# Own buffers for the weights a layer's last tiles read twice, the next layer's first splits on VectorE, and four tiles by halves at the end of the first attention

## The chip, the cores and the metric

One core of a Trainium2 chip runs the whole program. The metric is device time in microseconds (us) for one execution, as the median of several; lower is better. The engines are TensorE (PE, with its weight loads PEld), VectorE (DVE), ScalarE (ACT), GpSimd (POOL) and SyncE (SP, which issues most of the DMAs). Each engine takes its instructions in the order in which the program lists them.

## What is computed

One sequence of 512 positions, model width 1024, fp32, goes through two layers and a third, hybrid layer. Every layer starts from a normed and modulated copy of `x`, and ends by adding a gated product to `x`:

```python
for i in range(2):
    h = rms_norm(x, norm_mix[i]) * (1 + sc1) + sh1
    y = chunked_relpos_attention(h, ...) if i == 0 else chunked_spatial_gating(h, ...)
    x = x + g1 * y
    h = rms_norm(x, norm_ffn[i]) * (1 + sc2) + sh2
    x = x + g2 * squared_relu_mlp(h, ffn_w1[i], ffn_w2[i])      # hidden width 4096
return hybrid_layer(x, ...)      # block-sparse attention beside a state-space mixer, own norm at its start
```

So there are four layer ends inside the program, at which a norm over all of `x` stands between the last product of one half layer and the first product of the next: attention to feed-forward 0, feed-forward 0 to spatial gating, spatial gating to feed-forward 1, feed-forward 1 to the hybrid layer.

## The kernel before

`x` is held transposed as eight tiles `xT[k]` of 128 features by 512 positions. Every large product is made of three reduced-precision products (`mm3`, lines 147 to 152): each operand is split into a rounded part and its remainder, for activations `hH` and `hL`, for weights `wh` and `wl`. A weight chunk is read and split by `wchunk` (line 154): SP loads it into `raw` (four buffers), ScalarE rounds it into `wh` (line 163, three buffers), and VectorE or GpSimd subtracts to give `wl` (line 168, three buffers). Which of the two subtracts follows a running count, unless the caller names an engine.

At a layer's end `down_last` (line 336) makes the last four of eight output tiles. Tile 4 is made over all 512 positions. Tiles 5, 6 and 7 are made for the first 256 positions and then, from the same weights, for the other 256; so three `wh` and three `wl` buffers, which is all there are, stay taken until the second halves are done. `resid` (line 325) adds each product to `xT` on VectorE.

Into this is woven the next layer's norm, a generator (`norm`, line 249) that `down_last` steps: squares of the first five tiles on ScalarE (line 257) summed on GpSimd (line 261); for each half of the positions the squares of the last three (line 270) with two more sums (line 272), column sums by small products with ones (line 275), the mean (line 278), an inverse root `rsqrt` (line 171), two transposes that spread it over the partitions (line 282), and then `norm_tile` for each feature tile: line 315 on VectorE, line 316 on ScalarE (`hH`), line 317 on VectorE (`hL`). `rsqrt` is a bit trick and three Newton rounds, ten small VectorE instructions (lines 181 to 185); with `act=True` it is Ln and Exp on ScalarE (lines 178, 179) and one Newton round of three.

The next layer's first products are made by `up_first` (line 364) in steps of two feature tiles and a half of the positions, in the order SKEW (line 93): (0,0), (1,0), (0,1), (2,0), (1,1), (3,0), (2,1), (3,1). It splits four weight chunks, the first on VectorE and the other three on GpSimd. All four layer ends use both functions.

The order of instructions on each engine is set when the program is built, by a scheduler that simulates the engines and places what it thinks is ready, by priority; the norm's steps run at high priority. Buffers are rings: an instruction that writes one waits until its last readers are done. In the first attention `relb` and `P3` hold four position-bias tiles and four probability tiles; in the gating layer `v0` to `v3` hold the gated values; beside the second feed-forward the state-space tables are made in `s5_tab`, `s5_ct` and `s5_c9` and stored to DRAM (line 1003).

Of the kernel before, what the change touches and what calls it, by code (L numbers as in the profile page):

```python
# [19 lines left out]
T = 512  # L20
# [89 lines left out]
class Net:  # L110
# [42 lines left out]

    def wchunk(self, src, k, n, eng=None):

        nc = self.nc
        raw = self.wp.tile([128, 1024], F32, name="raw", tag="raw", bufs=4)
        wh = self.wp.tile([128, 1024], F32R, name="wh", tag="wh", bufs=3)
        wl = self.wp.tile([128, 1024], F32R, name="wl", tag="wl", bufs=3)
        v = lambda t: t[:, :k * n].rearrange("p (k n) -> p k n", k=k)  # L160
        for ap, o in (src if isinstance(src, list) else [(src, 0)]):
            nc.sync.dma_start(v(raw)[:, :, o:o + ap.shape[-1]], ap)
        nc.scalar.activation(wh[:, :k * n], raw[:, :k * n], AF.Copy)  # L163
        self.nsplit += 1
        if eng is None:
            pool = self.nsplit in FIRST_POOL if self.nsplit < 9 else self.nsplit % self.pmod == 0
            eng = nc.gpsimd if pool and self.pool_ok else nc.vector
        eng.tensor_tensor(wl[:, :k * n], raw[:, :k * n], wh[:, :k * n].bitcast(F32), op=ALU.subtract)  # L168
        return v(wh), v(wl)
# [78 lines left out]

    def norm(self, s1, sh, j):

# [3 lines left out]
        acc = None  # L254
        for k in range(KT - 3):
            sq = self.sp.tile([128, T], F32, name="sq", bufs=2)
            nc.scalar.activation(sq, self.xT[k], AF.Square)
            if acc is None:
                acc = sq
            else:  # L260
                add(acc, acc, sq, op=ALU.add)
        rb = [self.bank(t, (128, 256)) for t in "ot"]
        yield
        for hf in range(2):
            c0 = 256 * hf
            st = self.bank("c", (128, 2))
            a = acc[:, c0:c0 + 256]
            for k in range(KT - 3, KT):
                sq = self.sp.tile([128, 256], F32, name="sqh", bufs=2)
                nc.scalar.activation(sq, self.xT[k][:, c0:c0 + 256], AF.Square)  # L270
                if k < KT - 1:
                    add(a, a, sq, op=ALU.add)
# [5 lines left out]
            nc.vector.tensor_scalar(v, st, 1.0 / D, EPS, op0=ALU.mult, op1=ALU.add)  # L278
            r = self.rsqrt(v, [128, 2])
            yield  # L280
# [54 lines left out]

    def down_last(self, wr, parts, nk, gate, banks, norm):


        ws = {}
        for hf in (None, 0, 1):  # L340
            a, b = (0, T) if hf is None else (256 * hf, 256 * hf + 256)
            for m in (4,) if hf is None else (5, 6, 7):
                if m not in ws:
                    ws[m] = self.wchunk(wr[:, :, m * 128:m * 128 + 128], nk, 128)
                acc = self.bank(next(banks))[:, :b - a]
                for k in range(nk):
                    self.mm3(acc, [x[:, k, :] for x in ws[m]], [x[:, a:b] for x in parts(k)], k == 0, k == nk - 1)
                self.resid(m, gate[:, m:m + 1], acc, a, b - a)
                if hf != 0:
                    with self.tc.high_priority():  # L350
                        next(norm)
        with self.tc.high_priority():
            list(norm)
# [10 lines left out]
    def up_first(self, cols, banks, tokens=False):  # L364
# [3 lines left out]
        for kk, hf in SKEW:  # L368
            if hf == 0:
                ws[kk] = self.wchunk([(w[:, 2 * kk:2 * kk + 2, :], o) for w, o in cols], 2, 512,  # L370
                                      self.nc.gpsimd if kk > 0 else self.nc.vector)
            for k2 in range(2):
# [53 lines left out]
    def layer0(self):  # L426
# [4 lines left out]
        with ExitStack() as c:  # L431
# [88 lines left out]
            for m2 in range(2):  # L520
                list(out(m2, 1))
            self.down_last(w_out[:, 4:8, :], lambda k: (oH[4 + k], oL[4 + k]), 4, mod[:, 16:24],
                           itertools.repeat("a"), self.norm(self.s1[1], mod, 24))

# [107 lines left out]
    def then_layer1(self):  # L632
        self.scale1(2, 1, 8, "nmix1", 0, 8)
        self.scale1(3, 1, 32, "nffn1", 0, 8)
        return self.norm(self.s1[2], self.mods[1], 0)

# [4 lines left out]

    def ffn(self, l, then):
        nc, d, tc = self.nc, self.d, self.tc
# [3 lines left out]
        with ExitStack() as c:  # L647
# [32 lines left out]
            self.bg(100)  # L680
            self.down_last(w2[:, 24:32, :], lambda k: (gh[k], gl[k]), 8, mod[:, 40:48], banks, then())


    def layer1(self):
# [4 lines left out]
        with ExitStack() as c:  # L689
# [37 lines left out]
            for g in range(4):  # L727
# [28 lines left out]
                for m2 in range(4 if g < 3 else 2):  # L756
                    ws = [self.wchunk(w_out[:, g * 6 + 3 * hf:g * 6 + 3 * hf + 3, m2 * 256:m2 * 256 + 256], 3, 256)
                          for hf in range(2)]
                    self.down(m2, lambda k, mi: [x[:, k % 3, mi * 128:mi * 128 + 128] for x in ws[k // 3]],
                              lambda k: (gh[k], gl[k]), 6, mod[:, 16:24], banks)  # L760
            self.down_last(w_out[:, 18:24, :], lambda k: (gh[k], gl[k]), 6, mod[:, 16:24], banks,
                           self.norm(self.s1[3], mod, 24))

# [759 lines left out]
def body(tc, out, **d):  # L1523
    with ExitStack() as ctx:
# [10 lines left out]
        with tc.tile_pool(name="s5p", bufs=1) as sp5:  # L1535
# [3 lines left out]
            n.pool_ok = False  # L1539
            n.ffn(1, n.then_hybrid)  # L1540
            n.pool_ok = True
# [16 lines left out]
```

## Time and profile before

| what | value |
|---|---|
| median of 3 runs | 1873.36 us (1873.04 to 1874.86) |
| profiled execution | 1877.26 us, of which the span of instructions 1875.5 us |
| mean granted TensorE clock | 0.980 of full speed |
| TensorE busy | 1798.0 us, 96% of the span |
| VectorE, GpSimd, ScalarE busy | 1095.8, 664.8, 653.0 us |
| DMA | 243.07 MB, mean 130 GB/s |

Busy time of TensorE includes time at a lower granted clock, so a stretch can be full and slow at once; the granted clock stands in a column of its own in the views by stretch. The clock has two levels, 2.4 GHz (1.00) and 1.2 GHz (0.50); a figure between them is a stretch with both.

### The profile page before, as it was taken

Reading aid. Unit: us, or ns where it says so; the run is one execution under the profiler, and the core shown is the slowest. Engines: PE = TensorE matmul, PEld = TensorE weight load, DVE = VectorE, ACT = ScalarE, POOL = GpSimd, SP = SyncE. Lnnn points to the kernel's source line nnn. Section 1 sums busy time; section 2 is a strip of 40 time slices with the busy share of each in tenths; the row PEclk is TensorE's granted clock in tenths of the full one; section 3 lists DMA queues with packets and bytes.
Section 4 is the critical chain, followed back from the end, with each engine's and each line's share of the span. In section 5 each row is a group of like instructions: output and inputs, shape, how many; then the busy total and the mean of one; then the engine's idle time right before and its main releaser. Section 6 shows DMA issues by size and latency. Waiting matters only on the chain. (4 is left out here: it accounts for less than half of the span.)

```text
span 1875.5 us, 24762 instructions
## 1 busy us (share of the span) xinstructions
PE 1798.0 (96%) x9246; PEld 1433.0 (76%) x9246; DVE 1095.8 (58%) x2076; ACT 653.0 (35%) x1153; POOL 664.8 (35%) x714
## 2 busy tenths in 40 slices
PE   7999998998999999999999998998999999999999
PEld 3887765877788887888888888886888888786556
DVE  3366865888863336226333336996564554698773
ACT  2345444422332334233223233322232334234542
POOL 0266644121222232113222132038777531255341
PEclk9999999999999999999999999998999999999899
DMA  8553423467743323332322323663433354552101
GB/s 319 174 164 118 148 84 109 131 229 260 237 147 98 93 79 113 100 91 70 102 76 84 101 73 118 199 190 125 135 134 127 100 184 135 163 180 91 42 16 46
DMA packets 195801, 243.07 MB, mean 130 GB/s; under 512 B 18784, under 2 KB 147040, under 8 KB 194016
## 3 DMA queue, kind: packets, MB, share of 16 engines
q1 hardware_dynamic: 191712, 228.72, 38.7%
q10 hardware_dynamic: 3968, 12.76, 1.9%
q8 instruction: 73, 1.20, 0.3%
q14 instruction: 48, 0.39, 0.1%
HBM read 228.87 MB, written 12.58 MB: 129 GB/s over the span
## 5 line engine op out<-in xcount | busy, mean ns | idle before, releaser
L163 ACT ACTIVATE wh<-raw 128x1024 fp32r<-128x1024 f32 (+3 forms) x282 | 286.5, 1017 | 535.0 <-PE ps_a L151 141.5
L168 POOL TENSOR_TENSOR wl<-raw,wh 128x1024 fp32r<-128x1024 f32 (+3 forms) x90 | 210.4, 2338 | 695.4 <-ACT wh L163 685.2
L168 DVE TENSOR_TENSOR wl<-raw,wh 128x1024 fp32r<-128x1024 f32 (+3 forms) x192 | 240.2, 1252 | 212.5 <-ACT wh L163 211.1
L151 PE MATMUL ps_a<-hL,wh 128*128 128x512 f32 (+1 forms) x468 | 176.6, 379 | 3.1 <-DVE hL L317 2.7
L150 PE MATMUL ps_a<-hH,wh 128*128 128x512 f32 (+1 forms) x468 | 177.5, 389 | 1.9 <-ACT hH L316 1.1
L152 PE MATMUL ps_a<-hH,wl 128*128 128x512 f32 (+1 forms) x468 | 175.2, 377 | 3.2 <-DVE wl L168 3.2
L206 DVE SCALAR_TENSOR_TENSOR nrm_t<-araw,a_v,nrm_t 128x512 f32<-128x512 f32 x182 | 165.6, 914 | 20.3 <-DMA araw<-in_ada_w 12.0
L150 PE MATMUL ps_a<-wh,hH 128*128 128x256 f32 (+2 forms) x392 | 125.9, 323 | 5.1 <-ACT hH L316 4.8
L151 PE MATMUL ps_a<-wl,hH 128*128 128x256 f32 (+2 forms) x392 | 122.3, 312 | 0.9 <-POOL wl L168 0.9
L152 PE MATMUL ps_a<-wh,hL 128*128 128x256 f32 (+2 forms) x392 | 120.5, 312 | 0.0
L152 PEld LDWEIGHTS ps_a<-hH,wl 128*128 128x128 f32 x468 | 90.4, 193 | 19.9 <-DVE wl L168 3.6
L151 PEld LDWEIGHTS ps_a<-hL,wh 128*128 128x128 f32 x468 | 90.7, 194 | 19.3 <-DVE hL L317 3.6
L150 PEld LDWEIGHTS ps_a<-hH,wh 128*128 128x128 f32 x468 | 88.4, 193 | 19.7 <-issue 2.0
L151 PE MATMUL ps_s<-hL,wh 128*128 128x512 f32 (+1 forms) x288 | 103.3, 363 | 0.0
L152 PE MATMUL ps_s<-hH,wl 128*128 128x512 f32 (+1 forms) x288 | 103.0, 362 | 0.0
L150 PE MATMUL ps_s<-hH,wh 128*128 128x512 f32 (+1 forms) x288 | 99.8, 365 | 0.0
L152 PE MATMUL ps_t<-hH,wl 128*128 128x512 f32 (+1 forms) x248 | 96.4, 390 | 1.6 <-DVE wl L168 1.6
L150 PE MATMUL ps_t<-hH,wh 128*128 128x512 f32 (+1 forms) x248 | 97.0, 391 | 0.0
L151 PE MATMUL ps_t<-hL,wh 128*128 128x512 f32 (+1 forms) x248 | 96.7, 390 | 0.0
L150 PEld LDWEIGHTS ps_a<-wh,hH 128*128 128x128 f32 x392 | 74.4, 190 | 21.9 <-issue 11.0
L325 DVE SCALAR_TENSOR_TENSOR xT<-ps_a,mod,xT 128x512 f32<-128x512 f32 (+1 forms) x64 | 44.5, 698 | 77.3 <-PE ps_a L152 77.2
L151 PEld LDWEIGHTS ps_a<-wl,hH 128*128 128x128 f32 x392 | 74.7, 191 | 6.0 <-POOL wl L168 1.3
(494 smaller groups left out, 4281.2 us busy)
## 6 DMA issues: line engine op xcount, KB each, us to landing
raw<-in_ffn_w SPq DMA_DIRECT2D x128, 512.0 KB, 3.8
araw<-in_ada_w SPq DMA_DIRECT2D x28, 1024.0 KB, 5.3
raw<-in_b_w_in SPq DMA_DIRECT2D x48, 512.0 KB, 3.8
raw<-in_a_w_in SPq DMA_DIRECT2D x28, 512.0 KB, 4.7
araw<-in_ada_w SPq DMA_DIRECT2D x48, 256.0 KB, 3.2
raw<-in_b_w_out SPq DMA_DIRECT2D x32, 384.0 KB, 3.1
araw<-in_w_ada SPq DMA_DIRECT2D x48, 256.0 KB, 3.2
araw<-in_ada_w SPq DMA_DIRECT2D x16, 512.0 KB, 8.8
```

Source lines behind the costliest of these rows:

```text
L150: mm(out, ah, bh, start=start, stop=False)
L151: mm(out, ah, bl, start=False, stop=False)
L152: mm(out, al, bh, start=False, stop=stop)
L163: nc.scalar.activation(wh[:, :k * n], raw[:, :k * n], AF.Copy)
L168: eng.tensor_tensor(wl[:, :k * n], raw[:, :k * n], wh[:, :k * n].bitcast(F32), op=ALU.subtract)
L206: nc.vector.scalar_tensor_tensor(acc, v[:, i, :], cond[:, k:k + 1], acc, op0=ALU.mult, op1=ALU.add)
L325: self.nc.vector.scalar_tensor_tensor(x, acc, gate, x, op0=ALU.mult, op1=ALU.add)
```

## The change

Four edits. (1) `wchunk` takes its two result buffers from the caller, and `down_last` gives those for the tiles made by halves: at the end of the first attention the buffers of `P3` and `relb`, in the feed-forward 0 six new buffers `w_last`, in the gating layer parts of `v0` and `v1`, in feed-forward 1 parts of `s5_tab`, `s5_ct` and `s5_c9`. (2) All splits of `down_last` and of `up_first` subtract on VectorE. (3) At the end of the first attention tiles 4 to 7 are made by halves instead of 5 to 7 (`nh=4`). (4) The norms after the first attention and after feed-forward 0 take their inverse root by Ln and Exp (`act=True`).

```diff
@@ wchunk
-    def wchunk(self, src, k, n, eng=None):
+    def wchunk(self, src, k, n, eng=None, to=None):
         raw = self.wp.tile([128, 1024], F32, name="raw", tag="raw", bufs=4)
-        wh = self.wp.tile([128, 1024], F32R, name="wh", tag="wh", bufs=3)
-        wl = self.wp.tile([128, 1024], F32R, name="wl", tag="wl", bufs=3)
+        wh, wl = to or [self.wp.tile([128, 1024], F32R, name=n, tag=n, bufs=3) for n in ("wh", "wl")]
@@ norm
-    def norm(self, s1, sh, j):
+    def norm(self, s1, sh, j, nh=3, act=False):
-        for k in range(KT - 3):
+        for k in range(KT - nh):
-            for k in range(KT - 3, KT):
+            for k in range(KT - nh, KT):
-            r = self.rsqrt(v, [128, 2])
+            r = self.rsqrt(v, [128, 2], act)
@@ down_last
-    def down_last(self, wr, parts, nk, gate, banks, norm):
+    def down_last(self, wr, parts, nk, gate, banks, norm, hold, nh=3):
-            for m in (4,) if hf is None else (5, 6, 7):
+            for m in range(4, 8 - nh) if hf is None else range(8 - nh, 8):
                 if m not in ws:
-                    ws[m] = self.wchunk(wr[:, :, m * 128:m * 128 + 128], nk, 128)
+                    ws[m] = self.wchunk(wr[:, :, m * 128:m * 128 + 128], nk, 128, nc.vector,
+                                        None if hf is None else hold(m))
-                if hf != 0:
+                if hf is None and m == 7 - nh or hf == 1 and m in (8 - nh, 6, 7):
                     with self.tc.high_priority():
                         next(norm)
+            if hf is None and nh == 4:
+                with self.tc.high_priority():
+                    next(norm)
@@ up_first
-                ws[kk] = self.wchunk([(w[:, 2 * kk:2 * kk + 2, :], o) for w, o in cols], 2, 512,
-                                      self.nc.gpsimd if kk > 0 else self.nc.vector)
+                ws[kk] = self.wchunk([(w[:, 2 * kk:2 * kk + 2, :], o) for w, o in cols], 2, 512, self.nc.vector)
@@ layer0
+            hold = lambda m: [ap.tile([128, T], F32R, name="w" + t, tag=t, bufs=4) for t in ("P3", "relb")]
             self.down_last(w_out[:, 4:8, :], lambda k: (oH[4 + k], oL[4 + k]), 4, mod[:, 16:24],
-                           itertools.repeat("a"), self.norm(self.s1[1], mod, 24))
+                           itertools.repeat("a"), self.norm(self.s1[1], mod, 24, 4, True), hold, 4)
@@ then_layer1
-        return self.norm(self.s1[2], self.mods[1], 0)
+        return self.norm(self.s1[2], self.mods[1], 0, act=True)
@@ ffn
+            hold = hold or (lambda m: [fp.tile([128, 1024], F32R, name="w_last", bufs=6) for _ in range(2)])
-            self.down_last(w2[:, 24:32, :], lambda k: (gh[k], gl[k]), 8, mod[:, 40:48], banks, then())
+            self.down_last(w2[:, 24:32, :], lambda k: (gh[k], gl[k]), 8, mod[:, 40:48], banks, then(), hold)
@@ layer1
+            held = [t[:, i * 768:i * 768 + 768] for n in range(2)
+                    for t in [gp.tile([128, 3072], F32R, name=f"w_last{n}", tag=f"v{n}")] for i in range(4)]
+            hold = lambda m: [held.pop() for _ in range(2)]
@@ body, second feed-forward
+            held = []
+            def hold(m):
+                if not held:
+                    for t, w in (("tab", n.S5W), ("ct", 1152), ("c9", 1152)):
+                        x = sp5.tile([128, w], F32R, name="w_last_" + t, tag="s5_" + t)
+                        held.extend(x[:, i * 1024:i * 1024 + 1024] for i in range(w // 1024))
+                return held.pop(), held.pop()
-            n.ffn(1, n.then_hybrid)
+            n.ffn(1, n.then_hybrid, hold)
```

## Rows read from the trace of the kernel before

**Rows 1.** The page, part 1: busy us (share of the span) xinstructions.
```profile
PE 1798.0 (96%) x9246; PEld 1433.0 (76%) x9246; DVE 1095.8 (58%) x2076; ACT 653.0 (35%) x1153; POOL 664.8 (35%) x714
```

**Rows 2.** Waits of TensorE: waiter, what for: total us, times, longest.
```profile
PE ps_o L282 <- DVE rs_y L185: 7.5, 3, 6.0
```

**Rows 3.** Stretches: us, busy PE PEld DVE ACT POOL, PEclk, DMA, GB/s.
```profile
321.00:327.20 6.20, 0.17 (x2) 0.00 (x0) 5.90 (x10) 1.47 (x2) 4.69 (x3) 0.75 0.58 174
327.20:334.30 7.10, 7.10 (x33) 7.10 (x34) 4.56 (x19) 1.88 (x4) 0.00 (x0) 0.50 0.21 69
334.30:355.50 21.20, 20.69 (x172) 20.28 (x172) 16.91 (x30) 9.21 (x17) 3.87 (x2) 1.00 0.19 52
706.50:709.00 2.50, 1.30 (x9) 0.78 (x7) 2.19 (x5) 1.69 (x3) 2.50 (x3) 1.00 0.39 115
709.00:713.40 4.40, 4.40 (x15) 3.64 (x16) 4.23 (x10) 1.60 (x4) 1.85 (x2) 0.61 0.98 356
713.40:732.70 19.30, 17.94 (x77) 13.97 (x76) 14.35 (x33) 9.45 (x17) 2.40 (x1) 1.00 0.16 43
1139.20:1144.40 5.20, 0.23 (x2) 0.02 (x1) 5.10 (x7) 1.06 (x2) 4.50 (x3) 0.89 0.75 237
1144.40:1150.10 5.70, 5.68 (x27) 5.68 (x28) 4.92 (x22) 2.44 (x5) 0.00 (x0) 0.50 0.80 283
1150.10:1173.10 23.00, 21.42 (x179) 20.98 (x179) 15.58 (x41) 9.20 (x17) 2.39 (x1) 1.00 0.23 68
1533.10:1536.00 2.90, 1.87 (x14) 1.45 (x13) 2.60 (x6) 2.38 (x4) 2.90 (x6) 0.96 0.46 120
1536.00:1542.40 6.40, 5.14 (x24) 4.84 (x24) 5.31 (x18) 1.02 (x2) 1.46 (x1) 0.50 1.00 402
1542.40:1563.50 21.10, 20.60 (x172) 20.34 (x171) 13.31 (x26) 9.26 (x17) 6.77 (x6) 0.99 0.32 93
```

**Rows 4.** Timeline of VectorE, first layer end: start, us, instruction [idle before].
```profile
318.51 1.23 DVE L168 TENSOR_TENSOR wl<-raw,wh 128x1024 fp32r<-128x1024 f32 x1 [0.55 <-ACT wh L163]
...
320.43 2.30 DVE L183 TENSOR_TENSOR rs_t<-rs_y 128x2 f32<-128x2 f32 x1
...
326.02 0.14 DVE L183 TENSOR_TENSOR rs_t<-rs_y 128x2 f32<-128x2 f32 x1
326.20 0.16 DVE L184 SCALAR_TENSOR_TENSOR rs_t<-rs_t,st_v 128x2 f32<-128x2 f32 x1
...
342.28 2.72 DVE L317 SCALAR_TENSOR_TENSOR hL<-nrm_t,mod,hH 128x256 fp32r<-128x256 f32 x2 [1.07 <-ACT hH L316]
```

**Rows 5.** Timeline of GpSimd, same stretch.
```profile
318.80 1.54 POOL L272 TENSOR_TENSOR sq<-sq,sqh 128x256 f32<-128x256 f32 x1 [2.32 <-ACT sqh L270]
320.35 2.36 POOL L168 TENSOR_TENSOR wl<-raw,wh 128x1024 fp32r<-128x1024 f32 x1
322.67 0.72 POOL L272 TENSOR_TENSOR sq<-sq,sqh 128x256 f32<-128x256 f32 x1
```

**Rows 6.** Timeline of ScalarE, same stretch.
```profile
317.36 1.06 ACT L163 ACTIVATE wh<-raw 128x1024 fp32r<-128x1024 f32 x1 [0.29 <-PE ps_a L151]
```

**Rows 7.** ScalarE by line and shape, whole span: busy us, mean ns | idle.
```profile
L179 ACT ACTIVATE rs_y<-rs_t 128x16 f32<-128x16 f32 x8 | 1.7, 216 | 0.2
L178 ACT ACTIVATE rs_t<-a_v 128x16 f32<-128x16 f32 x8 | 1.7, 212 | 10.4 <-DVE a_v L561 10.4
...
L715 ACT ACT_TABLE_LOAD x1 | 1.3, 1283 | 0.0
```

**Rows 8.** The four stores of the state-space tables (line 1003), whole span.
```profile
L1003 ACTq DMA_DIRECT2D s5d<-s_tab x4: 326/330/332, 1337.4 to 1499.0; - x4
...
DMA to landing us min/median/max: 7.8/8.4/8.7
```

**Rows 9.** Waits of ScalarE, whole span.
```profile
ACT wh L163 <- DMA raw<-in_w_in: 26.8, 8, 11.4
```

**Rows 10.** Timeline of TensorE at the third layer end.
```profile
1155.31 0.50 PE L150 MATMUL ps_a<-hH,wh 128*128 128x256 f32 x2 [1.12 <-ACT hH L316]
```

More of the change, by code (lines that the diff above doesn't have):

```diff
@@ L334, in down @@
             self.resid(m, gate[:, m:m + 1], acc)
-    def down_last(self, wr, parts, nk, gate, banks, norm):
+    def down_last(self, wr, parts, nk, gate, banks, norm, hold, nh=3):
+        nc = self.nc
         ws = {}
@@ L639, in then_hybrid, with ffn @@
         return self.norm(self.s1[4], self.mods[2], 0)
-    def ffn(self, l, then):
+    def ffn(self, l, then, hold=None):
         nc, d, tc = self.nc, self.d, self.tc
@@ L760, in layer1 @@
                               lambda k: (gh[k], gl[k]), 6, mod[:, 16:24], banks)
+            held = [t[:, i * 768:i * 768 + 768] for n in range(2)
+                    for t in [gp.tile([128, 3072], F32R, name=f"w_last{n}", tag=f"v{n}")] for i in range(4)]
+            hold = lambda m: [held.pop() for _ in range(2)]
             self.down_last(w_out[:, 18:24, :], lambda k: (gh[k], gl[k]), 6, mod[:, 16:24], banks,
-                           self.norm(self.s1[3], mod, 24))
+                           self.norm(self.s1[3], mod, 24), hold)
     def tmp(self, pool, shape, name, bufs=1, dt=F32):
```

## Prediction

> **What bounds the kernel now.** I read the page's busy table first: TensorE is busy for 96% of the span [rows 1], so time can only be won where TensorE waits or runs slowly. The list of its waits comes next: its transposes on line 282, which spread the norm's inverse root, waited for VectorE three times, 6.0 us at the longest [rows 2]. Those transposes occur only at the four layer ends, so I read these by stretch [rows 3], three rows for each in order of time. I call them A (attention to feed-forward 0, 321.0 to 355.5), B (to gating, 706.5 to 732.7), C (to feed-forward 1, 1139.2 to 1173.1) and D (to the hybrid layer, 1533.1 to 1563.5); each begins where the last product of `down_last` ends and ends with `up_first`. A row's loss has two kinds: its length less its PE busy time (idle), and busy time at a granted clock under 1.00.
>
> Idle around the first half's statistics: A 6.20 - 0.17 = 6.03, B 2.50 - 1.30 = 1.20, C 5.20 - 0.23 = 4.97, D 1.03 + 1.26 = 2.29; together 14.49 us. Idle later in `up_first`: 0.51, 1.36, 1.58, 0.50; together 3.95. Clock: a product of 256 columns takes 20.69/172 = 0.120 us at 1.00 and 7.10/33 = 0.215 at 0.50, so busy time times (1 - clock) is lost: A 7.10 x 0.50 = 3.55, B 4.40 x 0.39 = 1.72, C 5.68 x 0.50 = 2.84, D 5.14 x 0.50 = 2.57; together 10.68. In all 29.1 us; A has 10.1, B 4.3, C 9.4, D 5.4 [rows 3]. The low clock follows the idle time each time; at B 1.20 us of idling, among products of one column, was enough.
>
> The cause is on two other engines. At A, VectorE's small instructions of the inverse root take 0.14 us and start 0.18 apart when nothing disturbs them (326.02, 326.20), but the same instruction took 2.30 at 320.43 [rows 4]. GpSimd's subtraction of a weight split ran from 320.35 for 2.36 [rows 5]: the VectorE instruction starts and ends with it. Both are there so late because the rounding on ScalarE waited for TensorE's last reads of the old weights (line 163 at 317.36, released by TensorE) [rows 6]: three buffers, all held for the second halves.
>
> **The change, part by part.** *Own buffers.* The tiles 5 to 7 no longer hold `wh` and `wl`, so the first three splits of `up_first` wait for chunks that are done before the halves begin. They can run in front of the statistics instead of among them. What it removes is the source of the 14.49 us. What it adds are waits for the borrowed buffers. P3 and relb are last read in the attention, v0 and v1 before the last output tiles of gating, w_last is new: no cost, as a tile or more of products hides each. At D tile 6 goes into `s5_tab`, whose last store is issued at 1499.0 and lands 8.4 us later, 1507.4 [rows 8]. Products of tile 6 begin five half tiles of 24 before 1533.1, at 1533.1 - 5 x 24 x 0.120 = 1518.7; less a rounding of 1.06 [rows 6] and a subtraction of 1.23 [rows 4] the split has to start by 1516.4, so 9 us of slack. If ScalarE's queue reached it at once, the rounding of weights needed sooner would stand behind it, and TensorE behind that: 0 to 8.4 us. I take 0, nearest to the slack.
>
> *Splits on VectorE.* Twelve subtractions of `up_first` go from 2.36 on GpSimd to 1.23 on VectorE [rows 4, 5]: 14.8 us more for an engine that is busy for 58% [rows 1]. Three of four at each end fall before the statistics and are hidden by the last tiles. The fourth falls within `up_first`; there GpSimd's split held line 317 at 342.28, a pair of 2.72 [rows 4], and TensorE's idle time in that stretch is 0.51 [rows 3]. Now 1.23 of VectorE's time comes instead: from a gain of 0.51 to a loss of 1.23 - 0.51 = 0.72 at an end; VectorE has 21.20 - 16.91 = 4.3 us free in that stretch, so I take 0. The splits of `down_last` that were GpSimd's move too, at least a tile ahead of use: 0.
>
> *Four tiles by halves at A.* The same columns in twice the products; weight loads are busy 20.28 beside 20.69 of products [rows 3], so they hide. Cost 0. It leaves three half tiles of 12 products after the first statistics, where there were two: 3 x 12 x 0.120 = 4.3 us of cover. At B and D two tiles of 24 give 5.8, at C two of 18 give 4.3. The sums on GpSimd grow by one of 0.72 [rows 5] for each half, ahead of the last tile's square: 0.
>
> *Ln and Exp at A and B.* Ten small instructions, 10 x 0.18 = 1.8 us, become 0.212 + 0.216 on ScalarE [rows 7] and 3 x 0.18: 0.97 us, with no load of a table, as the first load after the start is the 1.28 us one of gating's Gelu [rows 7]. At C and D 1.8 stays. All are shorter than their covers (4.3, 5.8, 4.3, 5.8).
>
> So the first idle time goes: 14.49. What is late next is the place of the transposes in TensorE's order. If they stand behind the last half tile, the way from them to the first product lies bare, as it does for the second half at C: 1.12 us [rows 10]. Bounds at each end are 0 and 1.12; at A and B, with the short root, I take 0, at C and D the middle, 0.6 each: 1.2 us. The second half's idle, 3.95, has the same cause and I count none of it as won (bounds: 0 to 3.95). The clock's 10.68 returns where the idle time goes; because B shows a fall after only 1.20 us, I leave one such loss, 1.72, in: 8.96.
>
> **Sum:** 14.49 - 1.2 + 8.96 = 22.3 us off the profiled execution, 1877.26 (span 1875.5 and 1.8 around it), which gives 1855.0. The median of the runs is 3.9 under that execution and has the same losses, I assume, so 1873.36 - 22.3 = **1851.1**.
>
> **Rivals.** (1) *VectorE's splits take GpSimd's place in the chain.* The scheduler may place them behind the mean. Three of 1.23 are 3.7; with the root 4.7 at A and B, 5.5 at C and D, against covers of 4.3, 5.8, 4.3, 5.8: new idle 0.4 and 1.2, and a low clock at A and C (3.55 + 2.84). The gain falls from 22.3 by 0.4 + 0.6 + 6.4 - 1.7 (already left in) = 5.7, to 16.6: 1856.8. For it: one split of VectorE stood in front of the mean at A (318.51) [rows 4]. Against: there is now nothing to wait for.
>
> The contention also runs the other way: GpSimd's sum at 318.80, beside VectorE's split of 318.51, took 1.54 instead of 0.72 [rows 4, 5], 0.82 more; two such sums on the way to each first statistic would make 8 x 0.82 = 6.6 us and 1857.7, which I count within this rival. The Trainium skill states it as a rule in its GPSIMD Engine Reference, section 8 (Key points): the engine shares its SBUF interfaces with VectorE and contends with VectorE's instructions that have two SBUF inputs, as a split has. By that rule each split moved to VectorE can hold a sum of the norm back; the trace agrees where the two met, and they meet less if the splits run early.
>
> (2) *The clock stays low.* The waits go, but the small products of statistics and transposes let the clock fall all the same, as at B after 1.20 us. Then 8.96 is not won: 22.3 - 9.0 = 13.3, 1860.1.
>
> (3) *It doesn't do what it says.* Loads still have only four raw buffers, and the order on each queue is fixed when the program is built; if the next layer's splits are placed as late as now, they keep their place and the root stays as slow for VectorE's own sake. Within 0.2%: some 1872.
>
> (4) *Slower: ScalarE's queue waits for loads.* A split that no longer waits for TensorE waits for its load, and the norm's squares stand behind it in ScalarE's order. Such waits exist: 8 times, 26.8 us, 3.35 in the mean and 11.4 at most [rows 9]. Three at each end are 10.05. The slack (cover less root) is 3.3, 4.8, 2.5, 4.0, so new idle time is 4 x 10.05 - 14.6 = 25.6, and the clock falls again (8.96): 1873.36 - 22.3 + 25.6 + 9.0 = 1885.7. It decides from about 7 us of such waits at each end (3.65 of slack and 13.3/4 of gain). Against it: loads come earlier too, since raw buffers are freed by the earlier splits.
>
> **How the numbers follow.** The forecast has 0.62, rival 1 0.14, rival 2 0.13, rival 3 0.06, rival 4 0.05. Faster by over 0.2% (3.7 us, about what a measurement of this kernel can tell from no change) are the first three: 0.89. Same 0.06, slower 0.05. The range reaches down to all 29.1 us won, 1844, and up past rival 2 by 3 us for the bounds of the borrowed buffers and the fourth split, 1863; it leaves out rivals 3 and 4 and a little of the rest, under 0.2 in all.
>
> **What would show it.** Right: at each end no VectorE instruction of the root over 1 us, no GpSimd split near it; roundings (line 163) of `up_first` before the second halves start; TensorE's wait for line 185 gone; granted clock 1.00 right behind the first transposes. Rival 1 shows as subtractions between the mean and the transposes, or sums of line 272 at 1.5; rival 2 as 0.50 without idle time; rival 4 as roundings released by loads just ahead of squares. I am wrong if the gain is not at A and C first (10.1 and 9.4 of the 29.1), or if a stretch far from the ends moves by over 3 us, since the order of instructions there was built anew as well.

## The result, and the profile after

The changed kernel takes 1850.49 us (median; 1846.26 to 1851.70), beside 1873.70 for the kernel before on the same chip: a ratio of 0.987 (95% interval 0.986 to 0.989), faster by 23.2 us. A second set, run later beside other kernels, gave 1848.55 and 0.985 (0.983 to 0.987). The forecast was 1851.1. That it came within 0.6 us is luck in part, since the two sets' medians lie 1.9 apart. The profiled execution took 1849.75 us with a span of 1847.9; that is 27.5 under the profiled execution of before, which lay 3.6 above its own median.

The page's first part of the changed kernel (to be held against [rows 1]): TensorE is busy for 9.1 us less with 12 products more, since fewer of them ran at the low clock, and GpSimd for 36 us less. VectorE, which the prediction gave 14.8 us more of splits, is busy for 3.7 less: by line its splits took 20 us more, but the root's instructions 18 less (28 of them are gone) and `hL` (line 316, before 317) 9.5 less.

```profile
PE 1788.9 (97%) x9258; PEld 1426.3 (77%) x9258; DVE 1092.1 (59%) x2065; ACT 653.5 (35%) x1162; POOL 628.9 (34%) x699
```

The four layer ends A, B, C, D as single stretches, the kernel before and then the changed one (columns as in [rows 3]):

```profile
299.00:356.00 57.00, 49.29 (x334) 45.29 (x331) 38.50 (x80) 22.70 (x40) 19.17 (x13) 0.91 0.36 113
690.00:733.00 43.00, 40.44 (x241) 35.09 (x241) 28.10 (x63) 17.44 (x31) 14.86 (x10) 0.96 0.29 89
1132.00:1173.20 41.20, 34.63 (x268) 33.98 (x268) 30.25 (x78) 15.95 (x28) 9.46 (x6) 0.92 0.37 117
1526.00:1563.50 37.50, 34.71 (x267) 33.71 (x267) 26.63 (x62) 15.40 (x27) 14.07 (x13) 0.91 0.43 145
```

```profile
299.00:349.50 50.50, 48.87 (x357) 45.16 (x355) 33.33 (x72) 20.47 (x41) 10.68 (x10) 1.00 0.39 126
677.40:715.30 37.90, 36.78 (x235) 32.94 (x234) 20.24 (x47) 14.08 (x30) 5.16 (x6) 1.00 0.19 58
1116.40:1152.90 36.50, 35.81 (x277) 34.92 (x276) 26.14 (x82) 12.87 (x25) 1.47 (x2) 0.95 0.30 98
1501.50:1537.00 35.50, 34.23 (x277) 33.19 (x277) 22.43 (x63) 12.51 (x24) 6.96 (x11) 1.00 0.34 112
```

Length less PE busy time is the idle time: 7.7, 2.6, 6.6, 2.8 us before, 1.6, 1.1, 0.7, 1.3 after. The granted clock is 1.00 at three ends where it was 0.91 to 0.96.

What became of the pieces is seen best at A. In the changed kernel, ScalarE rounds the next layer's second and third chunk at 302.39 and 308.66, before the half tiles and just as they begin (308.69), and its Ln and Exp take 0.19 and 0.20 us (timeline of ScalarE):

```profile
302.39 1.06 ACT L162 ACTIVATE wh<-raw 128x1024 fp32r<-128x1024 f32 x1 [2.23 <-PE ps_a L151]
...
308.66 1.06 ACT L162 ACTIVATE wh<-raw 128x1024 fp32r<-128x1024 f32 x1 [1.10 <-PE ps_a L151]
...
318.87 0.19 ACT L177 ACTIVATE rs_t<-st_v 128x2 f32<-128x2 f32 x1
319.09 0.20 ACT L178 ACTIVATE rs_y<-rs_t 128x2 f32<-128x2 f32 x1
```

VectorE's part of the root is done in 1.1 us, against [rows 4] where one of these instructions took 2.30 (timeline of VectorE):

```profile
319.32 0.47 DVE L182 TENSOR_TENSOR rs_t<-rs_y 128x2 f32<-128x2 f32 x1 [0.81 <-ACT rs_y L178]
319.83 0.16 DVE L183 SCALAR_TENSOR_TENSOR rs_t<-rs_t,st_v 128x2 f32<-128x2 f32 x1
...
320.30 0.15 DVE L184 SCALAR_TENSOR_TENSOR rs_y<-rs_t,rs_y 128x2 f32<-128x2 f32 x1
```

So TensorE's transposes follow the last half tile without a gap, and the first products come 1.7 us later; before, TensorE stood idle for 6.03 there [rows 3] (timeline of TensorE):

```profile
321.06 0.38 PE L281 MATMUL ps_o<-ident,rs_y 128*128 128x128 f32 x2
321.76 0.61 PE L274 MATMUL ps_c<-ones,sq 128*128 128x1 f32 x4 [0.32 <-POOL sq L271]
322.31 0.61 PE L274 MATMUL ps_c<-ones,sqh 128*128 128x1 f32 x4
322.77 0.49 PE L150 MATMUL ps_a<-hH,wh 128*128 128x256 f32 x2
```

### The profile page after: what moved, and what is told of

It is laid out like the page before. It is cut to its first block, busy times and chain, and to the rows that moved or that the text cites. A ratio compares the mean times of both kernels' runs of the same rounds, so it can differ in the third digit from the quotient of the medians.

```text
span 1847.9 us, 24744 instructions
## 1 busy us (share of the span) xinstructions
PE 1788.9 (97%) x9258; PEld 1426.3 (77%) x9258; DVE 1092.1 (59%) x2065; ACT 653.5 (35%) x1162; POOL 628.9 (34%) x699
## 5 line engine op out<-in xcount | busy, mean ns | idle before, releaser
L162 ACT ACTIVATE wh<-raw 128x1024 fp32r<-128x1024 f32 (+3 forms) x269 | 275.1, 1023 | 508.9 <-PE ps_a L151 130.6
L167 POOL TENSOR_TENSOR wl<-raw,wh 128x1024 fp32r<-128x1024 f32 (+3 forms) x74 | 172.6, 2333 | 652.5 <-ACT wh L162 649.5
L167 DVE TENSOR_TENSOR wl<-raw,wh 128x1024 fp32r<-128x1024 f32 (+2 forms) x195 | 245.8, 1261 | 218.0 <-ACT wh L162 216.1
L151 PE MATMUL ps_a<-hL,wh 128*128 128x512 f32 (+1 forms) x440 | 167.1, 382 | 1.2 <-DVE hL L316 0.8
L150 PE MATMUL ps_a<-hH,wh 128*128 128x512 f32 (+1 forms) x440 | 166.6, 389 | 1.7 <-ACT hH L315 0.8
L152 PE MATMUL ps_a<-hH,wl 128*128 128x512 f32 (+1 forms) x440 | 165.9, 381 | 2.2 <-DVE wl L167 2.2
L152 PEld LDWEIGHTS ps_a<-hH,wl 128*128 128x128 f32 x440 | 84.1, 191 | 18.6 <-DVE wl L167 2.6
L151 PEld LDWEIGHTS ps_a<-hL,wh 128*128 128x128 f32 x440 | 84.0, 191 | 16.7 <-DVE hL L316 1.2
L150 PEld LDWEIGHTS ps_a<-hH,wh 128*128 128x128 f32 x440 | 82.0, 191 | 19.3 <-issue 2.0
```

What stands on the lines that cost most here:

```text
L150: mm(out, ah, bh, start=start, stop=False)
L151: mm(out, ah, bl, start=False, stop=False)
L152: mm(out, al, bh, start=False, stop=stop)
```

## How the experiments are read

Executions of one kernel differ by up to 9.5 us, so medians alone can't place a loss. For each profiled execution the stretch view was read in pieces of 2.5 us; a stretch has lost its idle time (length less PE busy) plus its low clock (PE busy times one less granted clock). The table gives that loss by stretch, of one execution for each kernel; where the pieces fall moves it by some 0.2. An end is a wider stretch than in [rows 3]: with it, before loses 30.3 at the ends, of which [rows 3] have 29.1. The rest, 1.15, is three short waits at A (300 to 303 us) inside the attention's own products; they are in every kernel. "ffn0" and "ffn1" are the stretches between A and B and between C and D. "Ratio" is to the kernel before, run on the same chip; its medians there were 1873.70, then 1875.92, 1873.45 and 1876.43 for the three groups of four.

| kernel | median us | ratio (95%) | A | B | C | D | ends | ffn0 | ffn1 |
|---|---|---|---|---|---|---|---|---|---|
| before | 1873.70 | 1 | 11.3 | 4.2 | 9.3 | 5.5 | 30.3 | 10.6 | 11.4 |
| changed | 1850.49 | 0.987 (0.986-0.989) | 1.6 | 1.1 | 2.4 | 1.3 | 6.4 | 7.3 | 8.8 |
| hold_only | 1857.53 | 0.991 (0.989-0.992) | 6.3 | 2.0 | 4.1 | 1.8 | 14.1 | 8.7 | 11.7 |
| engine_only | 1862.53 | 0.993 (0.991-0.995) | 7.5 | 1.9 | 4.5 | 4.7 | 18.5 | 6.6 | 12.9 |
| root_ten_ops | 1850.79 | 0.988 (0.986-0.990) | 4.1 | 1.8 | 2.4 | 1.1 | 9.4 | 9.6 | 9.5 |
| three_halves | 1850.87 | 0.987 (0.985-0.989) | 3.5 | 1.1 | 2.4 | 1.4 | 8.3 | 8.8 | 6.5 |
| first_on_gpsimd | 1856.08 | 0.990 (0.988-0.992) | 2.0 | 1.4 | 1.2 | 1.7 | 6.3 | 11.7 | 10.5 |
| att_end_only | 1862.95 | 0.994 (0.993-0.996) | 1.6 | 4.2 | 9.0 | 4.7 | 19.5 | 9.1 | 11.4 |
| gate_halves4 | 1853.63 | 0.989 (0.988-0.991) | 1.7 | 1.1 | 1.9 | 1.3 | 6.0 | 8.0 | 7.9 |
| three_halves4 | 1857.62 | 0.991 (0.990-0.993) | 1.7 | 3.5 | 1.9 | 2.5 | 9.5 | 8.8 | 8.0 |
| changed_again | 1848.55 | 0.985 (0.983-0.987) | 1.6 | 1.1 | 0.7 | 1.5 | 5.0 | 9.1 | 9.0 |
| short_cover_long_root | 1853.49 | 0.988 (0.987-0.990) | 5.8 | 1.8 | 2.4 | 1.6 | 11.5 | 8.1 | 9.5 |
| halves_as_before | 1851.16 | 0.987 (0.985-0.989) | 1.6 | 1.1 | 0.7 | 1.4 | 4.9 | 8.0 | 9.2 |
| no_gpsimd_in_ffn0 | 1843.27 | 0.983 (0.981-0.985) | 1.6 | 1.1 | 0.7 | 1.4 | 4.9 | 3.0 | 8.9 |

## The experiments

**One part alone.** First only the buffers (hold_only), with the rest of the change undone:

```diff
-  2, 512, self.nc.vector)                       # up_first
+  2, 512, self.nc.gpsimd if kk > 0 else self.nc.vector)
-  nk, 128, nc.vector,                           # down_last
+  nk, 128, None,
-  self.norm(self.s1[1], mod, 24, 4, True), hold, 4)
+  self.norm(self.s1[1], mod, 24), hold)
-  self.norm(self.s1[2], self.mods[1], 0, act=True)
+  self.norm(self.s1[2], self.mods[1], 0)
```

> Only the buffers of their own for the weights read twice, at all four ends; the first splits of the next layer stay on GpSimd from the second chunk on, three tiles by halves everywhere, the ten-operation root everywhere. Theory (the splits fell among the first half's statistics because their buffers came free only when the second half tiles had been multiplied; early buffers move them ahead of the halves whatever engine does them): most of the gain, 16 to 21 us off the kernel before, 1853 to 1858 us, and no subtraction of the next layer's first weights between the first transposes and the first products. Rival (what hurt is GpSimd working beside VectorE's small operations and its own sums; early or late is second): under 7 us off, 1867 to 1874 us.

Then, in the kernel before, only the engine (engine_only):

```diff
-  2, 512, self.nc.gpsimd if kk > 0 else self.nc.vector)
+  2, 512, self.nc.vector)
```

> Only the next layer's first splits put on VectorE; nothing else of the change, so their buffers come free as late as before. Theory: the roundings on ScalarE and the subtractions, now 1.23 us each on VectorE where they were 2.36 on GpSimd, still fall among the first half's statistics, so a part of the gain, 5 to 12 us off, 1861 to 1869 us, with the wait of the first transposes for the root still in the list of waits though shorter. Rival (GpSimd beside VectorE is the cause): nearly all of it, 18 to 23 us off, 1851 to 1856 us.

The buffers alone won 18.4 us, the engine alone 13.4, a little over the theory's upper bound; the ends say 16.2 and 11.8 of the 23.9 that the whole change won there. So late release is the larger cause, and while it lasts the engine is more than a detail; the two gains overlap, since their sum is more than the whole. In engine_only rival 1 of the prediction stands in the trace: VectorE's own splits lie between the mean (line 278) and the last step of the root (timeline of VectorE at A, engine_only), and TensorE's wait for line 185 is still in the list of waits, 2.3 and 1.0 us (two buffers; second fence) where [rows 2] had 7.5.

```profile
322.45 0.15 DVE L278 TENSOR_SCALAR st_v<-ps_c 128x2 f32<-128x2 f32 x1
322.71 1.23 DVE L168 TENSOR_TENSOR wl<-raw,wh 128x1024 fp32r<-128x1024 f32 x1
323.85 0.69 DVE L181 TENSOR_SCALAR rs_y<-st_v 128x2 int32<-128x2 int32 x1
...
324.92 1.21 DVE L168 TENSOR_TENSOR wl<-raw,wh 128x1024 fp32r<-128x1024 f32 x1
326.06 0.15 DVE L184 SCALAR_TENSOR_TENSOR rs_t<-rs_t,st_v 128x2 f32<-128x2 f32 x1
```

```profile
PE ps_o L282 <- DVE rs_y L185: 2.3, 2, 1.5
...
PE ps_t L282 <- DVE rs_y L185: 1.0, 1, 1.0
```

In hold_only the splits are early, yet two stand in GpSimd's queue between its sums at A (timeline of GpSimd, hold_only), and the first half's sums end at 321.6. TensorE's transposes wait 0.85 us for the root, and the first products another 1.12 (second fence, TensorE). What the engine is worth with early buffers is read from short_cover_long_root below, which is hold_only with the splits on VectorE: there these sums end at 319.6 and the transposes don't wait, but the ends lose only 2.6 us less, 0.5 of it at A and 1.7 at C (the ratios are 0.988 and 0.991).

```profile
312.69 2.40 POOL L167 TENSOR_TENSOR wl<-raw,wh 128x1024 fp32r<-128x1024 f32 x1 [0.87 <-ACT wh L162]
315.04 1.31 POOL L260 TENSOR_TENSOR sq<-sq 128x512 f32<-128x512 f32 x1
316.29 2.41 POOL L167 TENSOR_TENSOR wl<-raw,wh 128x1024 fp32r<-128x1024 f32 x1
```

```profile
326.11 0.43 PE L281 MATMUL ps_o<-ident,rs_y 128*128 128x128 f32 x2 [0.85 <-DVE rs_y L184]
327.65 0.58 PE L150 MATMUL ps_a<-hH,wh 128*128 128x256 f32 x1 [1.12 <-ACT hH L315]
```

**The attention's end: root and cover.** Each of the two was undone alone, then both:

```diff
-  self.norm(self.s1[1], mod, 24, 4, True), hold, 4)
+  self.norm(self.s1[1], mod, 24, 4), hold, 4)      # root_ten_ops (and act=True gone at B)
+  self.norm(self.s1[1], mod, 24, 3, True), hold)   # three_halves
+  self.norm(self.s1[1], mod, 24), hold)            # short_cover_long_root (and at B)
```

> The whole change except that the root at the attention's end and at the first feed-forward's end is again made of ten operations on VectorE (1.8 us) and not of Ln and Exp with three (0.97 us). Theory: the second half tile's products cover either, so within 1.5 us of the changed kernel, 1849.5 to 1852 us. Rival (the shorter root is what took the idle time and with it the low clock away): 0.83 us more idle at each of two ends and the clock's loss there back, 3.55 at A and 1.72 at B, 1855 to 1858 us.

> The whole change except that three tiles and not four are cut into halves at the attention's end. Theory: the statistics of the first half then have one half tile less ahead of the first transposes but the same tiles behind the sums; 0 to 2.5 us over the changed kernel, 1850 to 1853 us, all of it at the attention's end. Rival (the longer run of half tiles is what carries A, since its tiles are the shortest, 12 products of 256 columns each): idle time of 2 to 3 us and the low clock's 3.55 us come back at A, 1855 to 1858 us.

> Three tiles by halves at the attention's end and the ten-operation root everywhere; the buffers of their own and all splits on VectorE are kept. Alone the long root cost 2.5 us of A's account and the fourth tile 1.8. Theory (each takes cover from the same chain, so they add or do worse): A loses 5.5 to 7 us where the changed kernel loses 1.6, nothing elsewhere over 1; 1853 to 1857 us. Rival (what A lost in those two runs was chance of one execution): A loses under 3.5 us, 1849 to 1852 us.

Each alone leaves the median at 1850.8 or 1850.9, within 0.4 us of the changed kernel's first set and 2.3 of its second, which is what this measurement can tell; both together give 1853.49, 4.9 above the unaltered changed kernel beside it. By the account A loses 2.5 (ten operations), 1.8 (three tiles) and 4.2 (both) more than the changed kernel's 1.6. But only 1.0, 0.2 and 1.1 of that is idle time; the rest is low clock behind it, and the last section shows that a low clock behind little idle time can be chance. So the theory of each run alone holds, and the pair costs more than either; how much of it is the clock's luck one profiled execution can't say. With both undone, the way from transposes to first products lies bare as in [rows 10], and the clock falls behind it, to 0.60 in 327.00 to 335.00 (timeline of TensorE at A, short_cover_long_root):

```profile
325.18 0.61 PE L274 MATMUL ps_c<-ones,sqh 128*128 128x1 f32 x4 [0.45 <-ACT sqh L269]
325.65 0.41 PE L281 MATMUL ps_o<-ident,rs_y 128*128 128x128 f32 x2
327.17 0.79 PE L150 MATMUL ps_a<-hH,wh 128*128 128x256 f32 x2 [1.11 <-ACT hH L315]
```

**Which splits the engine matters for.** The changed kernel with one of its two moves to VectorE undone:

```diff
-  2, 512, self.nc.vector)
+  2, 512, self.nc.gpsimd if kk > 0 else self.nc.vector)   # first_on_gpsimd
```

```diff
-  nk, 128, nc.vector,
+  nk, 128, None,                                          # halves_as_before
```

> The whole change except that the next layer's first splits stay on GpSimd from the second chunk on (9 of 2.40 us instead of 1.23 on VectorE); buffers of their own, four tiles by halves at the attention's end, the Ln and Exp root and the halves' own splits on VectorE are kept. Theory as mended by the run with the buffers alone (there two of these splits, at 312.69 and 316.29 us, stood in GpSimd's queue between its sums at the attention's end): the engine matters a little even when the splits come early, because GpSimd has the sums of squares too; 1 to 6 us over the changed kernel, 1851 to 1857 us, lost at A and C. Rival (with early buffers the engine is of no account, and the 7 us between the run with the buffers alone and the changed kernel are those of the halves' own splits and of the root): within 1 us of the changed kernel, 1849 to 1852 us.

> The whole change except that the splits of the weights read twice go to GpSimd or VectorE by turn as before, in their own buffers. Theory (they come so early, 10 us and more ahead of the sums, that the engine is of no account): ends within 1 us of the changed kernel's 6.4, 1848 to 1853 us. Rival (GpSimd's 2.40 us per split in front of its sums is what made the run with the buffers alone 7.8 us dearer at the ends): ends 3 us dearer or more, at A and C above all, 1853 to 1857 us.

The halves' splits are of no account at the ends: 4.9, as in the changed kernel's second execution; the median, 1851.16, is 2.6 above that kernel's beside it, which so few executions can't tell from nothing. The first splits are twelve, not the nine of the expectation (GpSimd has 74 of its large splits in this kernel, 62 in the changed one). Their time came as expected, 1856.08, but not for the reason: the ends lose 6.3, as in the changed kernel. The 5.6 us are elsewhere. In the profiled execution the low clock cost 4.5 more in the first 299 us, which lie ahead of everything that was moved; ffn0 lost 4.3 more and ffn1 1.7. One part of it is the move's: TensorE's wait for state-space tables that GpSimd makes in ffn1 (8.1 us before; first line below before, second the changed kernel, third first_on_gpsimd, from each one's list of waits):

```profile
PE ps_c L968 <- POOL s_B L963: 8.1, 1, 8.1
```

```profile
PE ps_c L978 <- POOL s_B L973: 3.1, 1, 3.1
```

```profile
PE ps_c L979 <- POOL s_B L974: 5.7, 1, 5.7
```

It was 7.6 and 8.5 with the buffers or the engine alone, 7.2 with the change at A alone, and 1.7 to 3.5 in the eight other kernels that have both parts. So the short wait takes buffers and VectorE together. Why those tables then come earlier against TensorE's work was not traced to one instruction; that stays open.

**One end alone.** All of the change at A, nothing at B, C and D (att_end_only):

```diff
-  2, 512, self.nc.vector)
+  2, 512, self.nc.gpsimd if kk > 0 and not first else self.nc.vector)   # first: layer 0
-  mod[:, 40:48], banks, then(), hold)      # both feed-forwards
+  mod[:, 40:48], banks, then())
-  self.norm(self.s1[3], mod, 24), hold)    # gating
+  self.norm(self.s1[3], mod, 24))
...
```

> All of the change at the attention's end (own buffers, four tiles by halves, Ln and Exp, splits of the first feed-forward's first weights on VectorE), nothing of it at the other three ends. Theory: each end is its own account, so A's losses fall from 11.25 us to under 2.5 and those of B, C and D stay within 1.5 us of what they were; 8 to 11 us off the kernel before, 1863 to 1868 us. Rival (time won at one end is lost at the next, since the weights' stream and the tables keep their own pace): B and C grow by 3 us or more, under 6 us off.

10.5 us came off; A lost 1.6 and the others 4.2, 9.0, 4.7, as they did before to within 0.9. An end is an account of its own: what is won there isn't given back later.

**More half tiles.** Four at C, and at B as well:

```diff
-  self.norm(self.s1[3], mod, 24), hold)
+  self.norm(self.s1[3], mod, 24, 4), hold, 4)                        # gate_halves4
-  name="w_last", bufs=6)                                              # three_halves4 has
+  name="w_last", bufs=8)                                              # these as well
-  banks, then(), hold)
+  banks, then(), hold, 4 - l)                                         # l: the layer, 0 or 1
-  self.norm(self.s1[2], self.mods[1], 0, act=True)
+  self.norm(self.s1[2], self.mods[1], 0, nh=4, act=True)
```

> The whole change and four tiles by halves at the gating's end too (C), where the changed kernel still has 0.69 us of idle time around the first half's statistics and, right behind them, a granted clock of 0.71 worth 1.66 us. Theory (the idle time lets the clock fall; one half tile more of cover of 18 products of 256 columns takes it away): C's losses fall from 2.35 to under 0.5, 2 us off the changed kernel, 1847 to 1850 us. Rival (the clock falls there for what TensorE does, one-column products among short halves, not for the idle time): the low clock stays at C, 1.4 us or more, and the time within 1 us of the changed kernel.

> Four tiles by halves at the gating's end (C), and at the first feed-forward's end too (B), where the changed kernel has 1.12 us idle between the second transposes and the products that need ScalarE's roundings, at a full clock. Theory: C as in the kernel with four there alone; at B the idle time stands behind the second transposes, not around the first half's statistics, so more half tiles don't reach it; B within 0.5 us, 1847 to 1850 us in all. Rival (longer runs of half tiles cover any wait at an end): B's idle time gone too, 1846 to 1849 us, or, if the second half's products come earlier than the third and fourth chunks' splits, B longer by over 1 us.

Neither won anything. C was expected to lose under 0.5 and loses 1.9: the 0.69 us around the statistics and the low clock are gone, but 1.93 us of idle time came in their place, behind the transposes of both halves (timeline of TensorE at C, gate_halves4):

```profile
1128.56 0.51 PE L150 MATMUL ps_a<-hH,wh 128*128 128x256 f32 x2 [0.65 <-ACT hH L315]
...
1136.70 0.50 PE L150 MATMUL ps_a<-hH,wh 128*128 128x256 f32 x2 [1.11 <-ACT hH L315]
```

At B, four halves made the second half's root late as well, 0.97 (three_halves4): B loses 2.4 us more, as the rival had it, though the wait is for the root and not for splits. The rest of the 7 us in its median isn't in the ends and was not placed; the profiled execution, 1854.05, was the fastest of its five.

```profile
705.79 0.43 PE L281 MATMUL ps_t<-ident,rs_y 128*128 128x128 f32 x2 [0.97 <-DVE rs_y L184]
707.34 0.80 PE L150 MATMUL ps_s<-wh,hH 128*128 128x512 f32 x1 [1.11 <-ACT hH L315]
```

**The changed kernel a second time, and a faster one.** no_gpsimd_in_ffn0 follows from what the other runs left: in ffn0, VectorE's sums stretch beside GpSimd's splits.

```diff
-  n.pmod = 2
+  n.pool_ok = False
   n.ffn(0, n.then_layer1)
-  n.pmod = 3
+  n.pool_ok = True
```

> The changed kernel unaltered, beside the three that follow. What is open: the stretches between the ends won 5.8 us (ffn0's body 3.3, ffn1's 2.5) that no step of the forecast has, and the low clock before the attention's end, where nothing is changed, cost 4.0 to 9.2 us from one profiled execution to the next. Theory (the ends' account repeats, the rest moves from execution to execution): the ends lose 6.4 us again, within 1, the low clock behind C's 0.69 us of idle time included; the bodies and the first 299 us move by some us; 1847 to 1854 us. Rival (the bodies' gain belongs to the change): ffn0's and ffn1's bodies lose 7.3 and 8.8 us again, within 1 each.

> The changed kernel with every split of the first feed-forward on VectorE (28 that GpSimd does in 2.41 us each go to VectorE at 1.22 each). VectorE is busy 207 of that stretch's 323 us and would be 241. For: a 128x512 operation of VectorE that takes 0.75 us took up to 2.97 there, and TensorE waits once for a GpSimd split (1.6 us of its 5.9 idle). Against: TensorE's other waits there, 4.3 us, are for VectorE's own splits. Theory (GpSimd's splits hold VectorE up and come late themselves): 1 to 4 us off the changed kernel, 1846 to 1850 us. Rival (VectorE's queue is what is late): ffn0's body loses 2 us more or up, 1852 to 1860 us.

Unaltered, the kernel's ends lost 5.0 where the theory said 6.4 within 1: the low clock behind C's idle time was not there this time. ffn0 lost 9.1 and not 7.3, so half of the 3.3 that it seemed to win is chance; ffn1's 9.0 repeats.

Without GpSimd's splits ffn0 loses 3.0, and the time is 1843.27, 5.3 under the changed kernel beside it, where 1 to 4 were expected, and 33 under the kernel before: the fastest of all (the intervals of the two ratios overlap by 0.0018). The stretch ffn0 of the changed kernel and of this one:

```profile
349.50:672.60 323.10, 317.18 (x1355) 253.73 (x1354) 206.95 (x288) 98.35 (x126) 71.45 (x31) 0.99 0.55 179
```

```profile
349.40:668.10 318.70, 315.69 (x1354) 253.05 (x1354) 213.79 (x315) 98.36 (x126) 3.07 (x3) 1.00 0.56 182
```

VectorE has 27 instructions more, at 1.22 us each 33 us, yet it is busy for only 6.8 us more, since its other instructions took 24 us less: it had spent that held up beside GpSimd. The largest part, 16.8 us, is one line (both kernels; duration ns min/median/max):

```profile
L205 DVE SCALAR_TENSOR_TENSOR nrm_t<-araw,a_v,nrm_t x92: 736/752/2965, 349.5 to 535.3; 128x512 f32<-128x512 f32 x92
```

```profile
L205 DVE SCALAR_TENSOR_TENSOR nrm_t<-araw,a_v,nrm_t x92: 710/746/755, 351.0 to 530.2; 128x512 f32<-128x512 f32 x92
```

This line has two inputs in SBUF, and its longest went from 2.97 us to 0.76. So the trace agrees with the rule that the prediction took from the Trainium skill (GPSIMD Engine Reference, section 8, Key points), that GpSimd contends with VectorE's instructions that have two SBUF inputs.

## Why the prediction was right, step by step

**The ends.** By the account they won, with the forecast's terms behind: A 9.6 (9.6), B 3.1 (1.2), C 7.0 (7.2), D 4.2 (4.3); 23.9 in all for 22.3. Two terms were put in the wrong place. The one low clock left in, 1.72, was priced at B: B ran at 1.00. C kept 1.66 in this execution and lost nothing to it in the next. The 0.6 us of idle time at C and D is right in size (0.48 + 0.21 at C, 0.66 at D), but at C it is not the place of the transposes: it is ScalarE's square of the second half (rows in the last section). And C's 7.0 beside 7.2 is two misses that cancel. The forecast counted none of the second halves' 3.95 us of idle time as won; C's 1.58 of it went, since the second transposes now stand among products (timeline of TensorE at C, the changed kernel; before, [rows 10]), and that pays for the 1.66 of low clock.

```profile
1131.37 0.28 PE L150 MATMUL ps_a<-hH,wh 128*128 128x256 f32 x1
1131.49 0.38 PE L281 MATMUL ps_t<-ident,rs_y 128*128 128x128 f32 x2
1131.62 0.37 PE L151 MATMUL ps_a<-hL,wh 128*128 128x256 f32 x1
```

**The cause.** Splits among the statistics, because their buffers came free late: shown by hold_only and engine_only. The prediction read the cause at A alone; the kernel before has it at the other ends too, an instruction of the root of 2.35 us at B, of 2.36 and 2.26 at C and of 2.32 at D, each beside a split of GpSimd (timelines of VectorE and GpSimd at C, the kernel before):

```profile
1138.37 2.36 DVE L184 SCALAR_TENSOR_TENSOR rs_t<-rs_t,st_v 128x2 f32<-128x2 f32 x1
```

```profile
1138.35 2.37 POOL L168 TENSOR_TENSOR wl<-raw,wh 128x1024 fp32r<-128x1024 f32 x1 [1.09 <-ACT wh L163]
```

The steps named as signs are there in the changed kernel: no split of GpSimd near the statistics at A, no operation of the root over 0.72 us at any end, roundings ahead of the second halves, the wait for line 185 gone from the list. The last sign, a granted clock of 1.00 behind the first transposes, holds at A, B and D, and at C in the second execution only.

**Costs taken as nothing.** Borrowed buffers, the fourth split and the fourth tile at A showed no loss of their own: of A's 1.6 us idle 1.15 was there before, ahead of the half tiles, and D's 1.3 are waits for `hH` and `hL`, not for a borrowed buffer. The short root and the fourth tile were costed as if either alone left cover enough, and by the medians it does; without both, A's cover is short.

**Rivals.** Rival 1 is real where the buffers come late (engine_only) and gone where they come early. Rival 2 happens by chance at C. Rivals 3 and 4 did not occur: the splits moved, and at A the roundings ahead of the second halves wait for TensorE, not for loads. ScalarE waits for loads ahead of the halves' own weights, 3.5 us at the longest (1474.04, ahead of D), and TensorE doesn't stand idle for it.

**What was missed.** The forecast said it would be wrong if a stretch far from the ends moved by over 3 us. One wait did: the one for the state-space tables in ffn1, 5.0 us shorter, with 2.1 us of VectorE's splits newly late in the same stretch, which as a whole moved by 2.5. (ffn0 moved by 3.3 in the first execution, by 1.5 in the second.) The wait belongs to the change (all kernels with both parts have it), and no step of the sum has it: the twelve subtractions were priced by what they cost VectorE and the statistics, not by what GpSimd's freed time would do for the tables behind them. With ends and ffn1 the account is 23.9 + 2.5 = 26.4 us, where the two comparisons of medians gave 23.2 and 27.9. The sum, 22.3, was low by 0.9 by the one and 5.6 by the other; both times lie inside the range.

## What to carry to other kernels

Ask of every buffer that is read twice what waits for its release, and what that work collides with when it is let go: here a rounding and a subtraction of the next layer, released too late, fell among the few small instructions that everything waited for. Moving work off an engine is worth pricing on both sides, what the receiving engine pays and what the relieved one, and an engine that it held up, get back; in ffn0 VectorE took on 33 us of work and was busy for 6.8 more. Where executions differ by more than an edit is worth, an account of idle time and low clock by stretch places a loss that the median can't.

## What the runs showed of the hardware that was not expected

**The same idle time lets the clock fall in one execution and not in the next.** At C, the changed kernel stood idle for the same 0.48 us, and 0.21 more, in both its profiled executions (timelines of TensorE, the first and the second execution):

```profile
1124.53 0.61 PE L274 MATMUL ps_c<-ones,sqh 128*128 128x1 f32 x4 [0.48 <-ACT sqh L269]
```

```profile
1126.23 0.61 PE L274 MATMUL ps_c<-ones,sqh 128*128 128x1 f32 x4 [0.48 <-ACT sqh L269]
```

Behind it the granted clock was 0.71 in the one and 1.00 in the other (stretches of 4.5 us, the same place in each; 0.71 is a stretch with both levels):

```profile
1127.00:1131.50 4.50, 4.50 (x30) 4.50 (x30) 1.89 (x10) 0.78 (x2) 0.00 (x0) 0.71 0.47 192
```

```profile
1128.70:1133.20 4.50, 4.50 (x41) 4.47 (x39) 2.83 (x13) 1.40 (x4) 0.00 (x0) 1.00 0.49 195
```

Of seven kernels whose C is that of the changed kernel, with 0.69 or 0.70 us of idle time there, four lost 1.66 to 1.70 us to it and three nothing; B's idle time, 1.1 to 1.8 us, cost nothing in any of them, so the prediction's reading that 1.20 us at B is enough is not a rule. The Trainium skill (TensorE: Matmul & The Clock Gate, Part 1) says of the clock's rise at the start of sustained work that its point differs from run to run, because the gate's own time base does not start with the kernel. The runs here agree that it differs, for the fall inside a kernel; they don't show the reason.

**Most of the spread between executions goes with the clock.** Over the 88 executions with a clock on record, each taken against the mean of its kernel in its group, time and mean granted clock have a correlation of -0.77, which is 0.60 of the variance. The profiled executions show where: before A, idle time was 25.8 to 27.8 us in every one of the fourteen, the low clock's loss 4.0 to 9.4. At some 105, 140 and 167 us the clock fell in some and not in others. At 105 the waits ahead of it weren't the same: the last of three was 0.69 to 0.76 us in seven executions, in all of which the clock fell, and 0.24 in the other seven, of which it fell in one. At 140 three waits of some 0.24, 0.69 and 0.76 us stand ahead in all fourteen, and it fell in seven; at 167 one of 1.75 stands ahead in all, and it fell in six. The place at 140 in halves_as_before, whose TensorE order up to there is that of the changed kernel, and in the changed kernel (for each the last wait, in the timeline of TensorE, and the stretch behind):

```profile
139.07 0.95 PE L539 MATMUL ps_t<-ident,rawq 128*128 128x128 f32 x5 [0.76 <-POOL rawq L570]
```

```profile
140.00:142.50 2.50, 2.50 (x14) 2.50 (x13) 0.73 (x2) 0.75 (x2) 2.04 (x6) 0.50 0.84 288
```

```profile
137.31 0.77 PE L539 MATMUL ps_t<-ident,rawq 128*128 128x128 f32 x5 [0.76 <-POOL rawq L570]
```

```profile
140.00:142.50 2.50, 2.50 (x18) 1.57 (x19) 0.45 (x2) 0.47 (x2) 1.00 (x4) 1.00 0.60 226
```
